# Gate loads in pieces, more load buffers, and sixteen experts kept on the chip, in a two-stage expert layer

## The chip, the cores and the metric

One core of a Trainium2 chip runs the program. The metric is the device time of one execution in microseconds (us). The kernel before took 3175.69 us in the median of three runs (3168.12 to 3179.25).

## The reference

A block of attention, recurrence and a PEER layer is followed by two further blocks (retention and stick-breaking attention, differential attention, each with a convolutional feed-forward part). All is float32, 512 tokens of width 1024. The change touches the PEER layer, which picks per token and head 16 of 16384 experts by two sets of 128 sub-keys:

```python
def block(t):
    q = (t @ wq).reshape(PEER_BLOCK, PEER_HEADS, 2, PEER_DQ // 2)
    s = jnp.einsum('tpcd,pckd->tpck', q, sub_keys).astype(jnp.float32)
    ...
    idx = jnp.take_along_axis(cidx, pos, axis=-1)
    g = jax.nn.softmax(top, axis=-1)
    a = jax.nn.gelu(jnp.einsum('tpkd,td->tpk', u[idx], t).astype(jnp.float32), approximate=False)
    return jnp.einsum('tpk,tpkd->td', (g * a).astype(t.dtype), v[idx])
```

## The kernel before, in words

The kernel doesn't gather for the first 384 tokens (`ND`). It computes all 16384 experts for them and weighs each with its gate, which is zero where the expert isn't picked. An "expert" below is a group of 128 experts; there are 128 of these, numbered 0 to 127. For the last 128 tokens (the "few") the picked rows of both tables are gathered, 128 rows for each table and token, one row per token and transfer: 256 gathers, issued by POOL into four `row` tiles, each with one DVE instruction (L1091 or L1103).

The layer has two stages.

*Hidden stage* (`experts`, `peer_hidden`). For each expert a 512 KB tile of `peer_u` is loaded raw (`wr`) and split into a high and a low float32r half (`wh` by ACT, `wl` by DVE; `wt`, L136). Three products of the halves give one float32 product (`mm3`): 24 matmuls of 128x128 by 128x384. ACT applies gelu (`gl`), and ACT's queue stores the tile of 128 hidden units by 384 tokens in DRAM (`hd`, 192 KB). Beside it the gates are worked out and stored in DRAM (`gd`) in 12 pieces of 32 tokens.

*Output stage* (`peer_out`). For each expert, in order, 192 KB of `hd` come back (`hx`, four buffers), every eighth expert also the gates of eight experts (`gs`, 1536 KB, two buffers). DVE multiplies (`hx<-hx,gs`), ACT and DVE split the product into `ah` and `al` (the trace calls both `ah`), the weights of `peer_v` are loaded and split like those of `peer_u`, and 24 matmuls add to eight accumulators that fill the whole of PSUM. The last three experts' products are kept until the end, where the few's sum is added and the next block's first weights are loaded (`group_start`).

What sets the order: a scheduler reorders the program's instructions ahead of time and gives each engine a fixed list. Each engine, and SP with the loads, works its list strictly in order, so that an instruction that waits holds up all behind it. A load waits until its buffer was read for the last time. Raw weights go round two buffers in the pool `w` and, in this layer, a third in the pool `few`; `wh` and `wl` have three buffers each, and so do `ah` and `al`. The few's DVE instructions are tied behind the split of the weights issued last (`paced`), which spreads them over the experts: 1.15 beside each hidden expert after the fourth, 1 beside each output expert.

Of the kernel before, what the change touches and what calls it, by code (L numbers as in the profile page):

```python
# [9 lines left out]
F32 = mybir.dt.float32  # L10
F32R = mybir.dt.float32r
# [8 lines left out]
P = 128  # L20
T = 512
L = 256
D = 1024
# [8 lines left out]
N2 = T // 2  # L32
TOKENS = (slice(0, N2), slice(N2, T))
SPARSE = 3
ND = 3 * P
HK = 32
HG_LEVELS = [64, 32, 16, 8, 4, 2, 1]
# [27 lines left out]
class Kern:  # L65
    def __init__(self, ctx, tc, A, out):
        self.ctx, self.tc, self.nc, self.A, self.out = ctx, tc, tc.nc, A, out
        self.table, self.epoch, self.later = None, [], []
        self.coming_up, self.ready, self.third, self.turn = [], [], None, 0
        self.pool = lambda name, bufs=1, **k: tc.tile_pool(name=name, bufs=bufs, **k)  # L70
        self.cst = ctx.enter_context(self.pool("cst"))
        self.wp = ctx.enter_context(self.pool("w"))
        self.hp = ctx.enter_context(self.pool("h"))
        self.sp = ctx.enter_context(self.pool("scr"))
        self.dp = ctx.enter_context(self.pool("dram", space=bass.MemoryType.DRAM))
        self.pp = ctx.enter_context(self.pool("ps", space=PSUM))
        self.psb = dict(mm=2, a=4, o=2)
# [58 lines left out]
    def wt(self, src):  # L136

        nc, n = self.nc, src.shape[-1]
        self.turn = (self.turn + 1) % 3
        third = self.third if self.turn == 0 else None  # L140
        raw = (third or self.wp).tile([P, 1024], F32, name="wr", tag="wr", bufs=1 if third else 2)[:, :n]
        hi = self.wp.tile([P, 1024], F32R, name="wh", tag="wh", bufs=3)[:, :n]
        lo = self.wp.tile([P, 1024], F32R, name="wl", tag="wl", bufs=3)[:, :n]
        nc.sync.dma_start(out=raw, in_=src)
        self.mark = self.split(raw, hi, lo)
        return hi, lo
# [776 lines left out]
    def peer_best(self, t, vals, idx):  # L923
# [59 lines left out]
        nc.vector.reciprocal(out=sm, in_=sm)  # L983
        if t != SPARSE:
            nc.vector.tensor_scalar(out=sm, in0=sm, scalar1=1024.0, scalar2=None, op0=ALU.mult)
# [3 lines left out]
    def peer_pick(self, t, vals, idx):  # L989
# [15 lines left out]
        return at, wt  # L1005

    def peer_gates(self, t, at, wt, gp, between):

        nc = self.nc
# [30 lines left out]
    def peer_hidden(self, e):  # L1040

        def evac(ps):
            g = self.fp.tile([P, ND], F32, name="gl", tag="gl", bufs=2)
            self.act(out=g, in_=ps, func=AF.Gelu)
            self.nc.scalar.dma_start(out=self.hd[e], in_=g)
        self.proj_t(self.A["peer_u"][e], [[x[:, :ND] for x in y] for y in self.h], evac, ND)

    def few_rows(self):

        nc = self.nc  # L1050
        tok = slice(ND, T)
        self.hn = self.fp.tile([P, D], F32, name="hn")
# [9 lines left out]
    def few_pick(self, vals, idx):  # L1062
        nc = self.nc
        ci = self.peer_best(SPARSE, vals, idx)
        self.few_i = self.fp.tile([P, P], U32, name="few_i")
# [45 lines left out]
    def peer(self):  # L1111
        nc, A = self.nc, self.A
        self.gd = self.dp.tile([ND // HK, P, P, HK], F32, name="gd")
        self.hd = self.dp.tile([P, P, ND], F32, name="hd")
        with self.pool("few") as self.fp:
            with self.pool("rt") as self.rt:
                self.iota = self.rt.tile([P, P], F16, name="iota")
                nc.scalar.dma_start(out=self.iota, in_=A["iota"])
                self.steps = self.rt.tile([P, 3, 16, 2], F16, name="steps")
                nc.scalar.dma_start(out=self.steps, in_=A["steps"])  # L1120
                vals, idx = self.peer_route()
                done, taken, few = [0], [0.0], iter(())

                def some(n):
                    taken[0] += n
                    while taken[0] >= 1:
                        taken[0] -= 1
                        next(few, None)

                def experts(upto):  # L1130
                    while done[0] < min(upto, P):
                        self.peer_hidden(done[0])
                        done[0] += 1
                        some(1.15)
                experts(4)
                self.few_rows()
                self.few_pick(vals, idx)
                few = self.few_experts()
                self.third = self.fp
                store = []  # L1140
                with self.pool("gp") as gp:
                    for t in range(3):
                        for k in range(4 if t else 10):
                            experts(done[0] + 1)
                            if store:
                                store.pop(0)()
                        at, wt = self.peer_pick(t, vals, idx)
                        base = done[0]
                        store = self.peer_gates(t, at, wt, gp, lambda k, base=base: experts(base + (28 * k) // P))
                    for k in range(4):  # L1150
                        experts(done[0] + 1)
                        store.pop(0)()
                experts(P)
            with self.pool("pv") as pv:
                self.peer_out(pv, few, some)

    def peer_out(self, pv, few, some):

        nc, A = self.nc, self.A
        acc = [self.ps(t) for t in ("a", "a", "a", "a", "o", "o", "mm", "mm")]  # L1160
        last = []
        for e in range(P):
            if e % 8 == 0:
                gs = pv.tile([P, ND // HK, 8, HK], F32, name="gs", tag="gs", bufs=2)
                nc.sync.dma_start(out=gs, in_=self.gd[:, :, e:e + 8, :].rearrange("t p i k -> p t i k"))
            h = pv.tile([P, ND], F32, name="hx", tag="hx", bufs=4)
            nc.sync.dma_start(out=h, in_=self.hd[e])
            w = self.wt(A["peer_v"][e])
            h4 = h.rearrange("p (t k) -> p t k", k=HK)
            self.mul(h4, h4, gs[:, :, e % 8, :])  # L1170
            a = [pv.tile([P, ND], F32R, name="ah", tag=t, bufs=3) for t in ("ah", "al")]
            self.split(h, *a)
            some(1.0)
            if e >= P - 3:
                last.append((w, a))
                continue
            for m in range(KD):
                self.mm3(acc[m][:, :ND], [(self.part(w, m), a)], start=e == 0, stop=False)
        self.run(few)
        self.third = None  # L1180
        self.h = self.htiles()
        s2 = self.scr("acc", T, 1)
        self.group_start([A["w_even"][i] for i in (16, 20, 17, 21)],
                         [[pv.tile([P, T], F32R, name="we", tag=t, bufs=4) for _ in range(4)] for t in ("we", "hx")])
        def column(m, c):
            x = self.x[m][:, c]
            d = slice(c.start, min(c.stop, ND))
# [611 lines left out]
```

## Time and profile before

| | |
|---|---|
| median of three runs | 3175.69 us |
| profiled execution | 3168.37 us, of which the span 3166.3 |
| PE busy | 3036.1 us, 96% |
| DVE, ACT, POOL busy | 70%, 46%, 13% |
| granted TensorE clock, mean | 0.981 |
| DMA over the span | 554.65 MB, 175 GB/s |
| last hidden gelu, first output matmul | 1281.5 us, 1280.5 us |
| last output matmuls before the kept three | 1857 us |

PE is TensorE's matmul, DVE is VectorE, ACT is ScalarE, SP is the engine whose queue issues the loads. An idle engine matters only where another waits for it. The granted clock is 1 at 2.4 GHz and 0.5 at 1.2 GHz.

### The profile page before, as it was taken

Reading aid. Unit: us, or ns where it says so; the run is one execution under the profiler, and the core shown is the slowest. Engines: PE = TensorE matmul, PEld = TensorE weight load, DVE = VectorE, ACT = ScalarE, POOL = GpSimd, SP = SyncE. Lnnn points to the kernel's source line nnn. Section 1 sums busy time; section 2 is a strip of 40 time slices with the busy share of each in tenths; the row PEclk is TensorE's granted clock in tenths of the full one; section 3 lists DMA queues with packets and bytes.
Section 4 is the critical chain, followed back from the end, with each engine's and each line's share of the span. In section 5 each row is a group of like instructions: output and inputs, shape, how many; then the busy total and the mean of one; then the engine's idle time right before and its main releaser. Section 6 shows DMA issues by size and latency. Waiting matters only on the chain.

```text
span 3166.3 us, 46312 instructions
## 1 busy us (share of the span) xinstructions
PE 3036.1 (96%) x17608; PEld 2740.4 (87%) x17608; DVE 2214.9 (70%) x4302; ACT 1465.6 (46%) x2291; POOL 399.0 (13%) x387
## 2 busy tenths in 40 slices
PE   7999999997999999999989999999999999999998
PEld 4998888887999998999989999778888887888887
DVE  7677767898988975677767664668664477786644
ACT  5654465333444443333333345766443277664433
POOL 0001210013333332222223100000000000000000
PEclk9999999998999999999999999999999999999999
DMA  6202444348989999988889832122333322223232
GB/s 221 67 28 81 144 159 134 103 147 286 330 326 343 338 354 349 317 304 308 312 290 322 272 115 80 60 61 84 98 99 93 94 86 79 77 76 99 93 98 82
DMA packets 199326, 554.65 MB, mean 175 GB/s; under 512 B 21280, under 2 KB 82208, under 8 KB 199104
## 3 DMA queue, kind: packets, MB, share of 16 engines
q1 hardware_dynamic: 137200, 376.36, 36.1%
q0 software_dynamic: 42608, 149.06, 13.6%
q10 hardware_dynamic: 19296, 26.28, 2.3%
q8 instruction: 138, 2.26, 0.3%
q14 instruction: 84, 0.69, 0.1%
HBM read 497.61 MB, written 54.00 MB: 174 GB/s over the span
## 4 chain that ended last, share of the span: by engine, by line
PE 64%; DMA 14%; DVE 14%; ACT 5%; issue 3%; SPq 0%; POOL 0%; DVEq 0%; ACTq 0%; POOLq 0%
PE mm L183 48%; DMA hx<-hd 8%; PE a L186 6%; PE a L183 4%; DVE wl L121 4%; PE o L186 2%; PE o L183 2%; DMA wr<-in_peer_u 2%; DVE row L1091 1%; ACT wh L109 1%; DMA wr<-in_w_mod 1%; ACT L105 1%; DMA wr<-in_peer_v 1%; DVE few_y L1103 1%; DVE ah L121 1%
## 5 line engine op out<-in xcount | busy, mean ns | idle before, releaser
L109 ACT ACTIVATE wh<-wr 128x1024 fp32r<-128x1024 f32 (+1 forms) x508 | 531.9, 1048 | 1068.5 <-PE mm L183 830.7
L121 DVE TENSOR_TENSOR wl<-wr,wh 128x1024 fp32r<-128x1024 f32 (+1 forms) x508 | 613.7, 1208 | 384.2 <-ACT wh L109 380.8
L183 PE MATMUL mm<-hh,wh 128*128 128x512 f32 (+2 forms) x2248 | 821.1, 368 | 23.2 <-ACT gl L109 20.6
L183 PE MATMUL mm<-hh,wl 128*128 128x512 f32 (+2 forms) x2216 | 806.4, 364 | 14.1 <-DVE wl L121 14.1
L183 PE MATMUL mm<-hl,wh 128*128 128x512 f32 (+2 forms) x2184 | 791.7, 363 | 0.0
L183 PEld LDWEIGHTS mm<-hh,wh 128*128 128x128 f32 x2248 | 426.4, 190 | 68.7 <-ACT gl L109 23.6
L183 PEld LDWEIGHTS mm<-hh,wl 128*128 128x128 f32 x2216 | 420.2, 190 | 59.2 <-DVE wl L121 16.6
L183 PEld LDWEIGHTS mm<-hl,wh 128*128 128x128 f32 x2184 | 414.1, 190 | 39.9 <-issue 1.0
L183 PE MATMUL a<-ah,wh 128*128 128x384 f32 (+1 forms) x1030 | 273.0, 345 | 34.3 <-DVE ah L121 34.3
L183 PE MATMUL mm<-ah,wh 128*128 128x384 f32 (+2 forms) x920 | 278.5, 349 | 1.0 <-DVE x L1239 1.0
L1084 POOL DMA_INDIRECT row<-in_peer_rows,few_i x128 | 167.9, 1312 | 570.1 <-DVE few_a L1091 255.5
L183 PE MATMUL mm<-ah,wl 128*128 128x512 f32 (+2 forms) x658 | 232.4, 353 | 0.0
L183 PEld LDWEIGHTS a<-ah,wh 128*128 128x128 f32 x1030 | 192.5, 194 | 38.9 <-DVE ah L121 38.5
L1084 POOL DMA_INDIRECT row<-in_peer_v,few_i x128 | 168.1, 1313 | 387.5 <-DVE few_y L1103 262.5
L121 DVE TENSOR_TENSOR hx<-hx,gs 128x384 f32<-128x384 f32 x128 | 71.0, 556 | 163.7 <-DMA hx<-hd 163.2
L183 PEld LDWEIGHTS mm<-ah,wh 128*128 128x128 f32 x920 | 171.2, 191 | 13.5 <-DVE x L1239 1.4
L183 PE MATMUL a<-ah,wl 128*128 128x384 f32 (+1 forms) x515 | 177.3, 344 | 0.0
L1103 DVE SCALAR_TENSOR_TENSOR few_y<-row,few_a,few_y 128x1024 f32<-128x1024 f32 x127 | 162.4, 1279 | 0.2
L1091 DVE CUSTOM_DVE_ANT_0 row<-row,hn 128x1024 f32<-128x1024 f32 x128 | 155.4, 1218 | 6.8 <-DMA row<-in_peer_rows,few_i 6.6
L183 PE MATMUL mm<-al,wh 128*128 128x512 f32 (+1 forms) x396 | 145.1, 366 | 0.0
L183 PE MATMUL o<-ah,wh 128*128 128x384 f32 (+2 forms) x524 | 135.9, 341 | 0.0
L183 PEld LDWEIGHTS mm<-ah,wl 128*128 128x128 f32 x658 | 124.9, 190 | 12.0
(491 smaller groups left out, 5554.0 us busy)
## 6 DMA issues: line engine op xcount, KB each, us to landing
wr<-in_peer_u SPq DMA_DIRECT2D x128, 512.0 KB
wr<-in_peer_v SPq DMA_DIRECT2D x128, 512.0 KB
wr<-in_w_up SPq DMA_DIRECT2D x88, 512.0 KB
hd<-gl ACTq DMA_DIRECT2D x128, 192.0 KB
gd<-gst SPq DMA_DIRECT2D x48, 512.0 KB
gs<-gd SPq DMA_DIRECT2D x16, 1536.0 KB
hx<-hd SPq DMA_DIRECT2D x128, 192.0 KB
wr<-in_w_mod SPq DMA_DIRECT2D x32, 512.0 KB
```

Source lines behind the costliest of these rows:

```text
L105: load = ins(self.nc.scalar.preload_act_table_set(name))
L109: i = ins(self.nc.scalar.activation(out=out, in_=in_, func=func, **k))
L121: return self.nc.vector.tensor_tensor(out=out, in0=a, in1=b, op=op)
L183: self.nc.tensor.matmul(ps, x, y, start=start and i == 0 and j == 0, stop=stop and i == n - 1 and j == 2, **kw)
L186: self.nc.tensor.matmul(ps, a, b, start=start, stop=stop, **k)
L1084: nc.gpsimd.indirect_dma_start(out=r, out_offset=None, in_=table, in_offset=bass.IndirectOffsetOnAxis(ap=self.few_i[:, k:k + 1], axis=0))
L1091: self.paced(nc.vector.tensor_tensor_reduce(out=r, in0=r, in1=self.hn, scale=1.0, scalar=0.0, op0=ALU.mult, op1=ALU.add, accum_out=dots[:, ...
L1103: self.paced(nc.vector.scalar_tensor_tensor(out=self.few_y, in0=r, scalar=dots[:, k:k + 1], in1=self.few_y, op0=ALU.mult, op1=ALU.add))
```

## The change

Gates: the first tile of eight experts is still loaded at once; each later one is loaded in four pieces of three token groups, issued in the program beside the fifth to eighth expert of the group before. The `hx` tile has six buffers instead of four. In the output stage raw weights go round four buffers, the fourth in the pool `pv`. The gelu outputs of experts 112 to 127 stay in a pool `hold` (16 tiles of 192 KB) and aren't stored or loaded; the output stage takes these 16 first, then 0 to 111. The next block's first weights go to the gathers' `row` tiles. The sum over experts is thus taken in another order, with the same terms.

```diff
     def wt(self, src):
...
-        self.turn = (self.turn + 1) % 3
-        third = self.third if self.turn == 0 else None
-        raw = (third or self.wp).tile([P, 1024], F32, name="wr", tag="wr", bufs=1 if third else 2)[:, :n]
+        pools = [self.wp, self.wp] + self.raws
+        pool = pools[self.turn % len(pools)]
+        self.turn += 1
+        raw = pool.tile([P, 1024], F32, name="wr", tag="wr", bufs=pools.count(pool))[:, :n]
...
     def peer_hidden(self, e):
 
         def evac(ps):
-            g = self.fp.tile([P, ND], F32, name="gl", tag="gl", bufs=2)
+            keep = e >= P - HELD
+            g = (self.hold if keep else self.fp).tile([P, ND], F32, name="gl", tag="gl", bufs=HELD if keep else 2)
             self.act(out=g, in_=ps, func=AF.Gelu)
-            self.nc.scalar.dma_start(out=self.hd[e], in_=g)
+            if keep:
+                self.held[e] = g
+            else:
+                self.nc.scalar.dma_start(out=self.hd[e], in_=g)
...
-                self.third = self.fp
+                self.raws = [self.fp]
...
+                experts(P - HELD)
+            with self.pool("hold") as self.hold:
                 experts(P)
-            with self.pool("pv") as pv:
-                self.peer_out(pv, few, some)
+                with self.pool("pv") as pv:
+                    self.peer_out(pv, few, some)
...
-        for e in range(P):
-            if e % 8 == 0:
-                gs = pv.tile([P, ND // HK, 8, HK], F32, name="gs", tag="gs", bufs=2)
-                nc.sync.dma_start(out=gs, in_=self.gd[:, :, e:e + 8, :].rearrange("t p i k -> p t i k"))
-            h = pv.tile([P, ND], F32, name="hx", tag="hx", bufs=4)
-            nc.sync.dma_start(out=h, in_=self.hd[e])
+        self.raws = [self.fp, pv]
+        order = list(range(P - HELD, P)) + list(range(P - HELD))
+        gates = {}
+
+        def gate_parts(p, ts):
+
+            if p not in gates:
+                gates[p] = pv.tile([P, ND // HK, 8, HK], F32, name="gs", tag="gs", bufs=2)
+            e = order[p]
+            nc.sync.dma_start(out=gates[p][:, ts], in_=self.gd[ts, :, e:e + 8, :].rearrange("t p i k -> p t i k"))
+        gate_parts(0, slice(0, ND // HK))
+        for p, e in enumerate(order):
+            if p % 8 > 3 and p + 8 < P:
+                gate_parts(p // 8 * 8 + 8, slice(p % 4 * 3, p % 4 * 3 + 3))
+            gs = gates[p // 8 * 8]
+            h = self.held.get(e)
+            if h is None:
+                h = pv.tile([P, ND], F32, name="hx", tag="hx", bufs=6)
+                nc.sync.dma_start(out=h, in_=self.hd[e])
             w = self.wt(A["peer_v"][e])
...
         self.group_start([A["w_even"][i] for i in (16, 20, 17, 21)],
-                         [[pv.tile([P, T], F32R, name="we", tag=t, bufs=4) for _ in range(4)] for t in ("we", "hx")])
+                         [[t[:, j * T:(j + 1) * T] for t in [self.fp.tile([P, D], F32R, name="we", tag="row", bufs=4) for _ in range(2)] for j in range(2)]
+                          for _ in range(2)])
```

How this moves instructions is shown at three places. Numbers behind names tell tiles apart; lines are those of the file each list comes from (a line after L136 of the old file has a higher number in the new one).

The first place is DVE's list where the first output products stand among the last hidden experts. Before, `hx_13106` is expert 0, `wl_12454` the split of hidden expert 111 and `wl_12491` that of 112:

```order
L121 TENSOR_TENSOR hx_13106<-hx_13106,gs_13104 128x384
L121 TENSOR_TENSOR wl_12454<-wr_12452,wh_12453 128x1024
L1091 ISA row_12486,few_a_6821<-row_12486,hn_6648 128x1024
L1091 ISA few_a_6821 128x1
L121 TENSOR_TENSOR ah_13116<-hx_13106,ah_13115 128x384
L121 TENSOR_TENSOR hx_13146<-hx_13146,gs_13104 128x384
L121 TENSOR_TENSOR hx_13186<-hx_13186,gs_13104 128x384
L121 TENSOR_TENSOR hx_13226<-hx_13226,gs_13104 128x384
L121 TENSOR_TENSOR wl_12491<-wr_12489,wh_12490 128x1024
```

In the changed list `wl_12606` is hidden expert 115, `gl_12524` the kept tile of 112:

```order
L122 TENSOR_TENSOR wl_12606<-wr_12604,wh_12605 128x1024
L1109 SCALAR_TENSOR_TENSOR few_y_6822<-row_12639,few_a_6821,few_y_6822 128x1024
L122 TENSOR_TENSOR gl_12524<-gl_12524,gs_13091 128x384
L122 TENSOR_TENSOR ah_13101<-gl_12524,ah_13100 128x384
L122 TENSOR_TENSOR gl_12560<-gl_12560,gs_13091 128x384
```

and later `gl_12781` is the kept tile of 119, the last to use the first gate tile `gs_13091`; `hx_13711`, `hx_13751` and `hx_13793` are experts 0 to 2 with the third gate tile `gs_13554`, and `wl_12971` is hidden expert 125:

```order
L122 TENSOR_TENSOR gl_12781<-gl_12781,gs_13091 128x384
L122 TENSOR_TENSOR wl_12899<-wr_12897,wh_12898 128x1024
L1109 SCALAR_TENSOR_TENSOR few_y_6822<-row_12930,few_a_6821,few_y_6822 128x1024
L122 TENSOR_TENSOR gl_12817<-gl_12817,gs_13245 128x384
L122 TENSOR_TENSOR wl_12935<-wr_12933,wh_12934 128x1024
L1109 SCALAR_TENSOR_TENSOR few_y_6822<-row_12966,few_a_6821,few_y_6822 128x1024
L122 TENSOR_TENSOR gl_12856<-gl_12856,gs_13245 128x384
L122 TENSOR_TENSOR hx_13711<-hx_13711,gs_13554 128x384
L122 TENSOR_TENSOR hx_13751<-hx_13751,gs_13554 128x384
L122 TENSOR_TENSOR hx_13793<-hx_13793,gs_13554 128x384
L122 TENSOR_TENSOR wl_12971<-wr_12969,wh_12970 128x1024
```

The first product moved from ahead of the split of 111 to behind that of 115; three products of later experts now stand ahead of the split of 125.

The second place is DVE's list in the middle of the output stage. Before, `ah_13396` is the low half of expert 7, `hx_13508` the product of expert 10 and `wl_13432` the weights of expert 8:

```order
L121 TENSOR_TENSOR ah_13396<-hx_13386,ah_13395 128x384
L1091 ISA row_13399,few_a_6821<-row_13399,hn_6648 128x1024
L1091 ISA few_a_6821 128x1
L121 TENSOR_TENSOR hx_13508<-hx_13508,gs_13426 128x384
L121 TENSOR_TENSOR wl_13432<-wr_13430,wh_13431 128x1024
L121 TENSOR_TENSOR ah_13438<-hx_13428,ah_13437 128x384
```

After, `ah_13761` is the low half of expert 1, `hx_13957` the product of expert 6 and `wl_13797` the weights of expert 2:

```order
L122 TENSOR_TENSOR ah_13761<-hx_13751,ah_13760 128x384
L1109 SCALAR_TENSOR_TENSOR few_y_6822<-row_13766,few_a_6821,few_y_6822 128x1024
L122 TENSOR_TENSOR hx_13957<-hx_13957,gs_13554 128x384
L122 TENSOR_TENSOR wl_13797<-wr_13795,wh_13796 128x1024
L122 TENSOR_TENSOR ah_13803<-hx_13793,ah_13802 128x384
```

Behind the split of expert e stands the product of e+3 before and of e+5 now.

The third place is SP's list in the output stage. Before, `hx_13428` and `hx_13468` are experts 8 and 9, `wr_13430` and `wr_13470` their weights, `gs_13748` the gates of 16 to 23:

```order
L1167 DMA hx_13428<-hd_5653 128x384
L1165 DMA gs_13748<-gd_5652 128x12x256
L144 DMA wr_13430<-in_peer_v 128x1024
L1167 DMA hx_13468<-hd_5653 128x384
L144 DMA wr_13470<-in_peer_v 128x1024
```

After, `hx_14038` and `hx_14078` are experts 8 and 9, `wr_13959`, `wr_14000` and `wr_14040` the weights of 6, 7 and 8, `gs_14198` the gates of 16 to 23:

```order
L146 DMA wr_13959<-in_peer_v 128x1024
L1189 DMA hx_14038<-hd_5653 128x384
L1180 DMA gs_14198<-gd_5652 128x3x256 x2
L146 DMA wr_14000<-in_peer_v 128x1024
L1189 DMA hx_14078<-hd_5653 128x384
L1180 DMA gs_14198<-gd_5652 128x3x256 x2
L146 DMA wr_14040<-in_peer_v 128x1024
```

Between the same two hx, the whole gate tile stood before and two of its pieces stand now, the other two behind the next hx; weights follow one expert later behind hx.

## Rows read from the trace of the kernel before

**Rows 1.** The page's part 2: busy tenths in 40 slices of the span.

```profile
PE   7999999997999999999989999999999999999998
...
DMA  6202444348989999988889832122333322223232
```

**Rows 2.** Stretches: from:to, length, busy of PE PEld DVE ACT POOL, clock, DMA share, GB/s.

```profile
1183.00:1280.50 97.50, 90.31 (x509) 89.36 (x509) 58.77 (x66) 32.08 (x46) 27.92 (x25) 0.98 0.98 349
1280.50:1372.00 91.50, 88.37 (x499) 87.73 (x499) 64.25 (x92) 30.90 (x43) 19.43 (x21) 0.98 0.90 309
1372.00:1760.00 388.00, 357.62 (x1977) 354.11 (x1975) 269.39 (x360) 122.20 (x168) 97.97 (x82) 0.96 0.89 308
1760.00:1857.00 97.00, 96.21 (x538) 95.96 (x539) 63.86 (x83) 35.00 (x48) 7.93 (x6) 0.96 0.67 218
```

**Rows 3.** Chain that ended last, late output stage: start, us, what.

```profile
1776.23 2.08 PE a L183 x12
...
1780.39 2.08 PE a L183 x12
```

**Rows 4.** Waits from 1280 to 1857: total us, times, longest.

```profile
DVE hx L121 <- DMA hx<-hd: 148.3, 57, 9.8
ACT wh L109 <- DMA wr<-in_peer_v: 95.4, 24, 9.2
...
PE a L183 <- DVE ah L121: 34.3, 13, 5.2
```

**Rows 5.** SP's queue of transfers in time: start, us to issue, engine, what.

```profile
1332.45 0.37 SPq L1165 DMA_DIRECT2D gs<-gd  x1
1333.59 1.16 SPq L144 DMA_DIRECT2D wr<-in_peer_v  x1
1334.80 1.17 SPq L1167 DMA_DIRECT2D hx<-hd  x1
...
1347.73 0.33 SPq L144 DMA_DIRECT2D wr<-in_peer_v  x1
```

**Rows 6.** Chain that ended last, output stage: waits for hx alone.

```profile
1334.80 11.12 DMA hx<-hd
1355.49 5.27 DMA hx<-hd
1362.97 5.01 DMA hx<-hd
...
1746.19 12.36 DMA hx<-hd
```

**Rows 7.** DVE in time; in brackets the idle time before.

```profile
1338.11 0.55 DVE L121 TENSOR_TENSOR ah<-hx,ah 128x384 fp32r<-128x384 f32 x1
...
1346.01 0.56 DVE L121 TENSOR_TENSOR hx<-hx,gs 128x384 f32<-128x384 f32 x1 [6.20 <-DMA hx<-hd]
1346.48 1.22 DVE L121 TENSOR_TENSOR wl<-wr,wh 128x1024 fp32r<-128x1024 f32 x1
```

**Rows 8.** Stretches as in rows 2: DMA share and GB/s at the end.

```profile
1100.00:1180.00 80.00, 80.00 (x557) 78.58 (x556) 63.06 (x69) 33.87 (x53) 28.36 (x21) 1.00 0.96 346
...
1334.00:1343.00 9.00, 9.00 (x54) 9.00 (x53) 4.48 (x8) 2.95 (x4) 1.87 (x2) 1.00 1.02 360
1346.00:1350.00 4.00, 2.63 (x15) 2.31 (x15) 3.99 (x7) 0.29 (x1) 0.42 (x1) 1.00 0.40 107
1355.00:1374.00 19.00, 19.00 (x111) 19.00 (x110) 16.82 (x21) 7.24 (x11) 4.83 (x5) 1.00 0.98 337
```

**Rows 9.** Waits from 1183 to 1280.5, the last hidden experts.

```profile
DVE hx L121 <- DMA hx<-hd: 14.8, 3, 8.8
...
PE mm L183 <- ACT gl L109: 7.2, 3, 3.7
```

**Rows 10.** Transfers of hx: issue time in ns, min/median/max, first and last.

```profile
L1167 SPq DMA_DIRECT2D hx<-hd x128: 319/341/2008, 1191.6 to 1841.4; - x128
```

**Rows 11.** What SP's queue waited for, 1280.5 to 1760.

```profile
SPq L144 <- DVE wl L121: 318.0, 90, 11.4
```

More of the change, by code (lines that the diff above doesn't have):

```diff
@@ L34 @@
 SPARSE = 3
+HELD = 16
 ND = 3 * P
@@ L68, in __init__ @@
         self.table, self.epoch, self.later = None, [], []
-        self.coming_up, self.ready, self.third, self.turn = [], [], None, 0
+        self.coming_up, self.ready, self.raws, self.turn = [], [], [], 0
         self.pool = lambda name, bufs=1, **k: tc.tile_pool(name=name, bufs=bufs, **k)
@@ L1113, in peer @@
         self.gd = self.dp.tile([ND // HK, P, P, HK], F32, name="gd")
-        self.hd = self.dp.tile([P, P, ND], F32, name="hd")
+        self.hd = self.dp.tile([P - HELD, P, ND], F32, name="hd")
+        self.held = {}
         with self.pool("few") as self.fp:
@@ L1173, in peer_out @@
             some(1.0)
-            if e >= P - 3:
+            if p >= P - 3:
                 last.append((w, a))
@@ L1177, in peer_out @@
             for m in range(KD):
-                self.mm3(acc[m][:, :ND], [(self.part(w, m), a)], start=e == 0, stop=False)
+                self.mm3(acc[m][:, :ND], [(self.part(w, m), a)], start=p == 0, stop=False)
         self.run(few)
-        self.third = None
+        self.raws = []
         self.h = self.htiles()
```

## Prediction

> **What bounds the kernel now.** I read the page first. PE is busy 96% of the span; its slices say 9 nearly everywhere, and from the tenth to the 23rd of 40 the DMA slices say 8 or 9 as well [rows 1]. In that part lies what the change touches; so I cut it by stretches: the last hidden experts (1183 to 1280.5 us), and the output experts in three pieces up to 1857 [rows 2]. In the output stage one expert costs PE 24 matmuls, and where nothing disturbs it the pattern comes back after 1780.39 - 1776.23 = 4.16 us [rows 3]. 125 experts run in it (three are kept for the end): 125 x 4.16 = 520 us, but it takes 576.5. The excess of about 56 us is the stake. The stretches say the same: idle PE is 3.1 + 30.4 + 0.8 = 34.3 us, and the granted clock of 0.98, 0.96 and 0.96 takes 0.02 x 91.5 + 0.04 x 388 + 0.04 x 97 = 21.2 us more; together 55.5. The last hidden experts lose 7.2 us idle and 0.02 x 97.5 = 1.9 us of clock [rows 2]. All that this change touches is worth at most 55.5 + 9.1 = 64.6 us.
>
> What the lost time waits for is in the list of waits: PE waits 34.3 us for the split of the hidden activations on DVE, and DVE waits 148.3 us, 57 times, for hx, the hidden activations that come back from DRAM; ACT waits 95.4 us for raw weights [rows 4]. The queue of SP tells why hx is late: a gate load of 1.5 MiB is issued at 1332.45, a weight load behind it, and hx behind both at 1334.80 [rows 5]. It is landed 11.1 us later; between two gate loads it takes 5.0 to 5.3 [rows 6]. DVE stands still for 6.20 us, and the weights' split behind it, for which PE waits next, stands too [rows 7]. From the first such pair of gate load and late hx to the last is 1746.19 - 1334.80 = 411.4 us for 11 groups of eight experts: 37.4 us a group, where PE alone wants 8 x 4.16 = 33.3.
>
> While DVE stands, nothing is issued: the next weights go out at 1347.73, nine us after the pair before [rows 5], and the DMA engines fall from a share of 1.02 and 360 GB/s to 0.40 and 107 [rows 8]. The stage is thus not short of bandwidth all the time; it runs full, then empty.
>
> **The change part by part.** Per output expert the transfers are 524 KB of raw weights, 197 of hx, 1573 / 8 = 197 of gates and 524 of gathered rows, 1.44 MB. At 4.16 us that is 347 GB/s. Between 1100 and 1180 the same engines moved 346 GB/s with PE busy all the 80 us [rows 8]. So PE's own pace can just be fed, if the engines never run empty. That is the knife's edge of this forecast.
>
> *Held experts.* 16 stores and 16 loads of hx go away, 3.1 MB each way, and the stage begins with the experts whose activations are in SBUF, with six hx already loaded. The first 22 experts need no hx in time; they want 1.25 MB in 4.16 us, 299 GB/s, below what any saturated row shows. They run at PE's pace and cover 22 x 4.16 = 91.5 us, just the length of the second stretch, which loses 3.1 + 1.8 = 4.9 us now. Gain 5.
>
> *The passage from hidden to output experts.* Before, DVE stood for hx for 14.8 us among the last hidden experts, and PE lost 7.2 us to a gelu queued behind [rows 9]. The order shows the first gate product moved from ahead of expert 111's weight split to behind 115's, some 16 us later, when its gate tile, issued at the same place, has landed. New are three hx products ahead of expert 125's split; they need the third gate tile, whose pieces can go out only after the eighth held product, about two experts before. Its 1.57 MB and one weight load are 2.1 MB beside gathers of 126 GB/s (524 KB each 4.16 us): 2.1 MB at 360 - 126 = 234 GB/s is 9 us, and the two experts are 8.3. So DVE may stand 1 to 4 us, with what a load takes to land, but PE needs that split only two experts later. On the other side two gate tiles, a weight load and six hx (4.9 MB) now sit in SP's queue among hidden experts 112 to 117 where 4.5 MB sat. I take 4 of the 9.1 us as staying (bounds 0 and 9.1). Gain 5.
>
> *Six buffers for hx.* The order eats them: before, the product of expert e+3 stood behind the split of e, now that of e+5 does. hx still goes out when one split is done and is wanted after the next; the slack is one expert, as before. I give this part nothing.
>
> *The fourth raw buffer.* Weights go out four experts ahead instead of three, 4.16 us more slack. The 95.4 us of ACT [rows 4] mostly lie beside DVE's wait for hx, so by itself I price it at nothing; it keeps work in the queue while DVE stands.
>
> *Gates in pieces.* Two pieces each go out behind two successive hx, 786 KB a time, instead of 1573 KB once. hx then has 2.2 us (at 360 GB/s) ahead of it twice, not 4.4 once. More to the point, when the first delayed hx lands, the second pair of pieces and a weight load are still queued, 1.3 MB or 3.6 us of work, so that the hole of [rows 8] should close. Group time: between gate loads DVE goes through two experts in 1362.97 - 1355.49 = 7.48 us, 3.75 each [rows 6], DVE's limit with hx in time; eight of them and the gates' full 4.4 us make 34.4 us, 1.1 above PE's 33.3. Of 256 gathers, 1.15 went beside each of 124 hidden experts, so that they run out near the 113th output expert, and 92 experts, 11.5 groups, remain behind the first 22: 13 us idle. DVE enters with the lead that three buffers for split weights allow, two experts or 8.3 us, and that covers most of it: 5 us. Clock has cost 21.2 us to 34.3 idle, 0.62 each, so 5 to 13 idle become 8 to 21 us. I take 11, nearer the end with the lead. Now the third and fourth stretch lose 30.4 + 15.5 + 0.8 + 3.9 = 50.6: gain 40. Ends: nothing lost (gain 50.6) and, with the group at 37.4 still, no gain.
>
> 45 more gate transfers are issued (1 + 15 x 4 against 16), 16 hx fewer. An issue takes SP 0.34 us, 2.0 at most [rows 10], and SP waited 318 us of that stage for DVE's splits [rows 11]: hidden.
>
> The Trainium skill ("DMA: Bandwidth & Descriptors", Rules for kernel authors) asks for at least 1 MiB per DMA, and its Anatomy section fits 2.0 us fixed per transfer; pieces of 384 KiB go against that, and 45 of them in line would be 90 us (an estimate from that page). In the stretch from 1355 to 1374, which has no transfer above 512 KiB, the engines moved 337 GB/s [rows 8], so that the fixed part evidently overlaps here; by this the pieces cost 1573 KB x (1/337 - 1/360) = 0.3 us a group.
>
> *Behind the stage* the first weights of the next block go into the gather buffers instead of hx buffers; these are free when the gathers end, 50 us before. Nothing.
>
> **Sum.** The profiled execution took 3168.4 us (span 3166.3 and 2.1 around). 3168.4 - 5 - 5 - 40 = 3118.4. The median shown, 3175.7, lies 7.3 above it; if that comes from this stage it goes, if from elsewhere it stays. I add half: 3122.
>
> **Rivals.**
> 1. *Smoother, but still short of data* (0.25). 347 GB/s is wanted throughout and the output stretches had 308; mixed with gates of 1 KB runs the engines may not hold it, and DVE, in order, still meets each hx one expert after its issue. A group comes half way, 35.4 us: 50.6 becomes 20 of gain, 3168.4 - 30 + 4 = 3142.
> 2. *The pieces do nothing* (0.11). hx waits for as many bytes, twice half instead of once the whole, and the group stays at 37.4. Only held experts and the passage gain: 3168.4 - 10 + 4 = 3162. Against it: the hole of [rows 8].
> 3. *Slower* (0.06). Each added piece holds SP's queue ahead of weights and hx. If each costs there the 2.0 us of the longest issue seen [rows 10], 45 x 2.0 = 90 against 50 of gain: 3168.4 + 40 + 4 = 3212. It decides from 1.3 us apiece; against it stand the 0.34 median and SP's long waits. The fixed part on that page of the Trainium skill would give the same.
>
> **How the numbers follow.** The forecast has 0.58, with a range of its own from 3106 (losses gone but for a little) to 3138 (the lead unused and no gain in the passage). Least thinkable is 3168.4 - 64.6 = 3104. The range goes from there into the second rival, to 3155; outside remain most of the cases of 3162 and the slower one. A change of under 0.3%, 9.5 us, can't be told from none here. Faster: the forecast, rival 1 and a third of rival 2, 0.87; same 0.07; slower 0.06.
>
> **What would show it.** Right: from 1280 on PE steps of 4.16 us over 22 experts; a stage of 520 to 535 us; DVE's wait for hx at single waits of some 3 us instead of 6 to 10; no stretch of DMA share 0.4; clock at 1.0 nearly throughout; before 1183 us and behind the stage nothing new. Wrong: groups of 36 us or more with the DMA share at 0.95 (rival 1), with holes still there (rival 2), or SP busy issuing while DVE and ACT wait for weights (rival 3). The forecast falls altogether if the wait moves to the gathers, which DVE hardly waited for, or if the passage loses more than now.

## The result, and the profile after

The changed kernel takes 3132.9 us (median of four runs, 3130.9 to 3135.4), against 3175.2 for the kernel before on the same chip: a ratio of 0.9861, 95% interval 0.9840 to 0.9882. That is faster by 42 us, or 1.3%, and lies in the predicted range of 3104 to 3155, 11 us above the predicted 3122. The profiled execution took 3133.6 us, its span 3131.6. The gap of 7.3 us between profile and median of before is not there.

In the page's slices the columns are as in [rows 1]:

```profile
PE   7999999998999999999999999999999999999998
...
DMA  6212454238989999899999722222333232223332
```

In the output stage the DMA slices are now 9 from the 18th to the 22nd, where four of these five were 8. The stage by stretches, cut as in [rows 2] but at this kernel's own bounds (the stage runs from 1281.8 to 1821.6 us, 539.7 us against 576.4):

```profile
1183.00:1281.50 98.50, 93.98 (x530) 92.85 (x529) 64.19 (x76) 33.26 (x48) 31.24 (x24) 0.98 0.92 335
1281.50:1373.00 91.50, 91.50 (x530) 91.50 (x528) 66.55 (x92) 32.57 (x45) 23.89 (x23) 1.00 0.91 313
1373.00:1725.00 352.00, 340.37 (x1939) 336.68 (x1939) 266.03 (x355) 120.81 (x165) 87.79 (x81) 1.00 0.94 329
1725.00:1822.00 97.00, 95.84 (x551) 95.06 (x550) 61.89 (x79) 34.06 (x47) 5.71 (x6) 1.00 0.65 214
```

The second stretch now has PE busy without a gap at clock 1.00, where [rows 2] had 88.37 of 91.50 at 0.98. The third keeps an idle rest of 352 - 340.37 = 11.6 us (30.4 before) and the clock is 1.00 where it was 0.96. DMA share and rate rose from 0.89 and 308 GB/s to 0.94 and 329. The waits from 1281.5 to 1822 (total us, times, longest) answer to [rows 4]:

```profile
DVE hx L122 <- DMA hx<-hd: 102.5, 63, 4.4
...
PE a L185 <- DVE ah L122: 12.7, 12, 2.5
```

DVE's wait for hx fell from 148.3 to 102.5 us, and its longest from 9.8 to 4.4; the 95.4 us of ACT for raw weights are gone from the list, ACT now waits for PE (313.7 us); PE's own wait fell from 34.3 to 12.7. So the change did what it says, and did not finish: hx is still late, and the transfers still run empty at times, if seldom (columns as in [rows 2], against the 0.40 and 107 GB/s of [rows 8]):

```profile
1628.00:1632.00 4.00, 3.12 (x18) 2.80 (x17) 4.00 (x5) 1.93 (x4) 0.39 (x1) 1.00 0.31 77
```

SP's queue in a group of eight shows why hx is late (start, us to issue, what), beside [rows 5]:

```profile
1457.65 0.91 SPq L1180 DMA_DIRECT2D gs<-gd  x2
1458.79 0.35 SPq L146 DMA_DIRECT2D wr<-in_peer_v  x1
1459.25 0.60 SPq L1189 DMA_DIRECT2D hx<-hd  x1
1459.90 1.76 SPq L1180 DMA_DIRECT2D gs<-gd  x2
1462.15 0.34 SPq L146 DMA_DIRECT2D wr<-in_peer_v  x1
1462.61 0.35 SPq L1189 DMA_DIRECT2D hx<-hd  x1
```

All four pieces go out within 4 us, in two pairs, each pair with a weight load ahead of the next hx. In the program they belong to four successive experts; in SP's list, as the third place above shows, they stand two and two around a weight load and an hx, and they go out once the gate buffer comes free. The hx of 1462.61 lands 11.2 us later, just as long as in [rows 6], and DVE stands for it (in brackets the idle time before):

```profile
1473.90 0.56 DVE L122 TENSOR_TENSOR hx<-hx,gs 128x384 f32<-128x384 f32 x1 [4.33 <-DMA hx<-hd]
```

4.33 us instead of the 6.20 of [rows 7], but still in every group: from the 24th output expert's split to the 112th, eleven groups of eight, the trace has 386.2 us, 35.1 each (37.45 by the same count before).

Where the 34.7 us of span came from: the stage gave 36.7, the passage ahead of it 3, the first hidden expert's gelu came 4.5 us later in this execution than in the one of before, and what lies behind the stage took 0.6 us more. These are the two rows (kernel before, then after; first and last start stand at the end of the time columns), 628.9 us from first to last gelu before and 625.7 after:

```profile
L109 ACT ACTIVATE gl<-mm x128: 466/472/512, 652.6 to 1281.5; 128x384 f32<-128x384 f32 x128
```

```profile
L110 ACT ACTIVATE gl<-mm x128: 467/472/510, 657.1 to 1282.8; 128x384 f32<-128x384 f32 x128
```

Nothing that the change touches lies ahead of that first gelu; in the thirteen profiled executions here it comes between 649.6 and 658.5 us. Such a difference of a few us says nothing of the change, and stages are compared below instead of spans.

### The profile page after: what moved, and what is told of

The parts are those of the page before. It is cut to its first block, busy times and chain, and to the rows that moved or that the text cites. A ratio compares the mean times of both kernels' runs of the same rounds, so it can differ in the third digit from the quotient of the medians.

```text
span 3131.6 us, 46209 instructions
## 1 busy us (share of the span) xinstructions
PE 3023.7 (97%) x17608; PEld 2725.8 (87%) x17608; DVE 2216.3 (71%) x4302; ACT 1466.5 (47%) x2291; POOL 394.1 (13%) x387
## 3 DMA queue, kind: packets, MB, share of 16 engines
q1 hardware_dynamic: 135616, 373.22, 36.3%
## 4 chain that ended last, share of the span: by engine, by line
PE 71%; DMA 12%; DVE 10%; ACT 5%; issue 2%; POOL 0%; DVEq 0%; SPq 0%; ACTq 0%
PE mm L185 52%; PE a L188 7%; DMA hx<-hd 7%; PE a L185 5%; DVE wl L122 3%; PE o L185 3%; PE o L188 3%; DMA wr<-in_peer_u 1%; ACT wh L110 1%; DMA wr<-in_w_mod 1%; ACT L106 1%; DMA gs<-gd 1%; DVE ah L122 1%; DMA row<-in_peer_rows,few_i 1%; DVE row L1097 0%
## 5 line engine op out<-in xcount | busy, mean ns | idle before, releaser
L185 PE MATMUL a<-ah,wh 128*128 128x384 f32 (+1 forms) x1030 | 265.4, 336 | 12.8 <-DVE ah L122 12.7
L1090 POOL DMA_INDIRECT row<-in_peer_v,few_i x128 | 164.5, 1285 | 384.0 <-DVE few_y L1109 272.2
L185 PEld LDWEIGHTS a<-ah,wh 128*128 128x128 f32 x1030 | 186.7, 189 | 17.5 <-DVE ah L122 16.9
L1109 DVE SCALAR_TENSOR_TENSOR few_y<-row,few_a,few_y 128x1024 f32<-128x1024 f32 x127 | 162.5, 1280 | 0.4 <-DMA row<-in_peer_v,few_i 0.3
L122 DVE TENSOR_TENSOR hx<-hx,gs 128x384 f32<-128x384 f32 x112 | 62.2, 558 | 109.9 <-DMA hx<-hd 102.5
L185 PE MATMUL mm<-wh,hl 128*128 128x256 f32 x464 | 133.3, 287 | 0.0
```

The source lines that it names most:

```text
L122: return self.nc.vector.tensor_tensor(out=out, in0=a, in1=b, op=op)
L185: self.nc.tensor.matmul(ps, x, y, start=start and i == 0 and j == 0, stop=stop and i == n - 1 and j == 2, **kw)
L1090: nc.gpsimd.indirect_dma_start(out=r, out_offset=None, in_=table, in_offset=bass.IndirectOffsetOnAxis(ap=self.few_i[:, k:k + 1], axis=0))
L1109: self.paced(nc.vector.scalar_tensor_tensor(out=self.few_y, in0=r, scalar=dots[:, k:k + 1], in1=self.few_y, op0=ALU.mult, op1=ALU.add))
```

## Experiments

The first four take the change apart. The other seven test why hx is late and what it costs. Each was timed beside the kernel before, whose median was 3172.1 to 3175.9 us; kernels are therefore compared by their ratios to it. Stages are read from one profiled execution each. A common ruler for the stage is the stretch from 1400 to 1700 us, in which PE, if never kept waiting, is busy 300 us at clock 1.00 (columns as in [rows 2]); in the kernel before, and then in the changed one, it reads

```profile
1400.00:1700.00 300.00, 277.02 (x1525) 274.47 (x1524) 209.93 (x289) 94.56 (x130) 75.63 (x64) 0.95 0.88 306
```

```profile
1400.00:1700.00 300.00, 289.13 (x1646) 285.85 (x1645) 227.57 (x311) 101.66 (x139) 71.83 (x69) 0.99 0.94 327
```

**Pieces alone.** The kernel before, with only the gates' loads cut:

```diff
+        gate_parts(0, slice(0, ND // HK))
...
-            if e % 8 == 0:
-                gs = pv.tile([P, ND // HK, 8, HK], F32, name="gs", tag="gs", bufs=2)
-                nc.sync.dma_start(out=gs, in_=self.gd[:, :, e:e + 8, :].rearrange("t p i k -> p t i k"))
+            if e % 8 > 3 and e + 8 < P:
+                gate_parts(e // 8 * 8 + 8, slice(e % 4 * 3, e % 4 * 3 + 3))
+            gs = gates[e // 8 * 8]
```

> The kernel before with the gates in four pieces and nothing else changed: no held experts, four hx buffers, three raw buffers. Theory (smaller gate loads close the hole in the transfers): a group of eight output experts falls from 37.4 us to about the 35.1 of the changed kernel, over some 12 groups 25 to 28 us, so 3147 to 3150, between 3140 and 3158; DVE's wait for hx falls from 148 to about 105 us. Rival 1 (the fourth raw buffer made the gain): with three raw buffers it stays above 3165. Rival 2 (the held experts made it, by 3.1 MB less each way and a lead): also above 3165.

Measured 3146.3 us, ratio 0.9914 (0.9896 to 0.9933). Its waits in the output stage:

```profile
ACT wh L109 <- DMA wr<-in_peer_v: 98.2, 29, 5.9
...
PE a L183 <- DVE ah L121: 16.9, 15, 2.2
```

The pieces alone halve PE's wait (34.3 to 16.9) and leave ACT's wait for raw weights where it was. DVE's wait for hx fell to 123.5 us, less far than the 105 expected; the group came to about 35 us as expected, and the stage to 546.6 from 576.4. The pieces alone thus give some 29 of the 42 us.

**The rest without the pieces.** The changed kernel with whole gate loads:

```diff
-            if p % 8 > 3 and p + 8 < P:
-                gate_parts(p // 8 * 8 + 8, slice(p % 4 * 3, p % 4 * 3 + 3))
+            if p % 8 == 0:
+                gate_parts(p, slice(0, ND // HK))
```

> The changed kernel with each gate tile loaded whole again, ahead of the first expert of its group; held experts, six hx buffers and four raw buffers stay. Theory: the first 22 experts still run at PE's pace and the groups behind go back to about 37.4 us, so that some 25 of the 42 us are lost: 3155 to 3160. Rivals 1 and 2 (raw buffer or held experts): 3135 to 3142, and groups stay near 35 us.

Measured 3150.1 us, 0.9928 (0.9910 to 0.9945), 17 us above the changed kernel, some 25 below before, and below the expected range: held experts and buffers give more than expected. The parts don't add up, 29 and 25 against 42 for both, so that the pieces are worth 29 us put in first and 17 put in last.

```profile
DVE hx L122 <- DMA hx<-hd: 113.2, 52, 8.6
...
PE a L185 <- DVE ah L122: 22.6, 12, 3.6
```

hx's longest wait is 8.6 us again, as it is with whole gates; the group is 36.3 us.

**Three raw buffers.**

```diff
-        self.raws = [self.fp, pv]
+        self.raws = [self.fp]
```

> The changed kernel with three raw weight buffers instead of four. Theory: weights were late only behind a whole gate tile; the time stays at 3133 to 3138. Rival 1 (the fourth raw buffer made the gain): ACT's wait for raw weights returns to some 95 us and the time to 3150 or more.

Measured 3137.8 us, 0.9881 (0.9859 to 0.9903).

```profile
ACT wh L110 <- DMA wr<-in_peer_v: 90.7, 27, 6.4
...
PE a L185 <- DVE ah L122: 11.7, 9, 2.0
```

ACT's wait comes back to 90.7 us, and PE's stays at 11.7. A long wait of an engine that another wait covers is worth little: 5 us at most, with intervals that overlap, and 2 us of stage (541.9 against 539.7).

**Four hx buffers.**

```diff
-                h = pv.tile([P, ND], F32, name="hx", tag="hx", bufs=6)
+                h = pv.tile([P, ND], F32, name="hx", tag="hx", bufs=4)
```

> The changed kernel with four hx buffers instead of six. Theory: DVE's order uses up the buffers, each hx is still wanted one expert after its issue, and the time stays at 3133, within 4 us. Rival (six buffers give hx the slack): DVE's wait for hx goes back towards 148 us and the time to 3145 or more.

A miss: 3123.6 us (3123.2 to 3126.0), 0.9841 (0.9823 to 0.9860), faster than the changed kernel in every single run. By the medians the two more buffers had cost 9 us; the intervals of the two ratios overlap a little, but the stage says the same, 532.4 against 539.7 us, and PE's wait in it fell from 12.7 to 6.8. DVE's wait for hx did not go up:

```profile
DVE hx L122 <- DMA hx<-hd: 95.1, 71, 5.0
```

SP's queue of this kernel in a group with pieces:

```profile
1463.57 0.34 SPq L146 DMA_DIRECT2D wr<-in_peer_v  x1
1464.04 0.53 SPq L1189 DMA_DIRECT2D hx<-hd  x1
1464.62 1.45 SPq L1180 DMA_DIRECT2D gs<-gd  x2
1468.40 0.33 SPq L1189 DMA_DIRECT2D hx<-hd  x1
1468.77 6.38 SPq L146 DMA_DIRECT2D wr<-in_peer_v  x2
```

Behind the second pair of pieces hx now goes ahead of its weight load (1468.40), where the changed kernel had a weight load between (1462.15, 1462.61). In the chain that ended last the late hx of the changed kernel reads, and then that of this one:

```profile
1462.61 11.19 DMA hx<-hd
```

```profile
1468.40 8.83 DMA hx<-hd
```

524 KB less ahead of it, and 2.4 us less from issue to landing in this pair; 1.1 of these are lost again, as hx was issued 3.8 us behind the second pair of pieces here and 2.7 us behind it there. Six buffers move the hx loads two experts up the list, past the weights of their own expert, without giving them more time before use. That the two orders differ so is shown; that this alone makes the 9 us is inferred, and the next runs bear on it.

**Is it the burst of pieces or the mean rate?** The four pieces of a group tied each behind another expert's hx load:

```diff
+            g = nc.sync.dma_start(out=gates[p][:, ts], in_=self.gd[ts, :, e:e + 8, :].rearrange("t p i k -> p t i k"))
+            if hx:
+                self.after(getattr(g, "ins", g), hx[-1])
...
-            if p % 8 > 3 and p + 8 < P:
-                gate_parts(p // 8 * 8 + 8, slice(p % 4 * 3, p % 4 * 3 + 3))
+            if p % 2 and p + 8 < P:
+                gate_parts(p // 8 * 8 + 8, slice(p % 8 // 2 * 3, p % 8 // 2 * 3 + 3))
```

> The changed kernel, but the four pieces of a gate tile are tied each behind the gelu load of another expert, so that one piece goes out every second expert, where in the changed kernel all four go out within two experts. Theory A (the burst of pieces makes two experts of each eight late, by 7 us in place of 4.16): the late experts vanish, groups 33.3 to 34.2 us, time 3113 to 3123. Theory B (the mean data rate binds, about 335 GB/s, wherever the pieces stand): groups 34.4 to 35.1, time 3123 to 3133.

Measured 3113.8 us, 0.9808 (0.9784 to 0.9831). SP's queue now has one piece for two experts, and the stretch from 1400 to 1700 and the waits read:

```profile
1456.93 0.42 SPq L1180 DMA_DIRECT2D gs<-gd  x1
...
1460.77 0.53 SPq L1191 DMA_DIRECT2D hx<-hd  x1
...
1465.50 0.34 SPq L1191 DMA_DIRECT2D hx<-hd  x1
1465.89 0.62 SPq L1180 DMA_DIRECT2D gs<-gd  x1
```

```profile
1400.00:1700.00 300.00, 299.08 (x1724) 298.44 (x1724) 235.28 (x319) 106.75 (x147) 84.58 (x72) 1.00 0.96 340
```

```profile
DVE hx L122 <- DMA hx<-hd: 82.1, 70, 4.4
...
PE a L185 <- DVE ah L122: 1.1, 3, 0.6
```

PE waits 1.1 us where it waited 12.7, at 340 GB/s. DVE still waits 82.1 us for hx, but only two of the waits in the stage are over 2.8 us, where the changed kernel has twelve. The mean rate was no limit; the burst was, for a product that wants its load one expert after its issue.

**The same with four hx buffers** (both edits above).

> The same spread pieces with four buffers for gelu outputs in place of six. Four buffers with the pieces close together gave 3123.6 against 3132.9 with six. If the fewer buffers are worth 9 us by themselves, this is some 9 us below the spread kernel with six; if they only changed how the pieces' burst met the other loads, both are the same within 3 us: 3113 to 3121.

Measured 3115.6 us, 0.9804 (0.9780 to 0.9828): the same as with six.

```profile
1400.00:1700.00 300.00, 300.00 (x1732) 300.00 (x1732) 241.38 (x323) 107.67 (x147) 78.66 (x72) 1.00 0.97 347
```

```profile
DVE hx L122 <- DMA hx<-hd: 60.2, 64, 3.3
```

This is less of a test than it was meant to be. With the pieces spread PE already runs at its own pace with six buffers (299.08 of 300 us busy), so that nothing was left to gain; and DVE's wait for hx did fall, from 82.1 to 60.2 us. That fewer buffers help only by how the burst meets the other loads fits the time, but isn't shown.

**Is it the place of the product?** The changed kernel with each gate product placed behind the split of its own expert's weights on DVE:

```diff
-            self.mul(h4, h4, gs[:, :, e % 8, :])
+            self.paced(self.tt(h4, h4, gs[:, :, e % 8, :], ALU.mult))
```

> The changed kernel, but each product of a gelu output with its gates is placed behind the split of its own expert's weight tile on VectorE, so that a gelu load has some six experts between issue and use in place of one. Theory A (each late load is a load wanted one expert after its issue, because the product stands early in VectorE's order): VectorE's waits for gelu loads nearly vanish (102.5 us in the changed kernel, under 30 here), the groups of eight come to 33.5 to 34.2 us, the time to 3117 to 3124 us. Theory B (the stage's data rate is the limit, the waits only show it): the waits go elsewhere, groups stay at 35.1, time 3130 to 3136. A third outcome, slower than 3136, if the later product, which also frees the gate tile later, makes the gate pieces late.

Measured 3113.3 us, 0.9802 (0.9779 to 0.9824), lower than either theory's range. DVE's wait for hx is not in the list any more, and no wait for raw weights is over 1.2 us in the stage:

```profile
ACT ah L110 <- DVE hx L122: 209.0, 110, 2.2
```

```profile
1400.00:1700.00 300.00, 300.00 (x1733) 300.00 (x1732) 240.96 (x323) 116.29 (x148) 73.53 (x72) 1.00 0.97 348
```

ACT now waits 209 us for the products, 2.2 at a time at most, DVE waits for ACT's halves in turn (91.2 us from 1282 to 1800), and PE waits for neither: it is busy for all of the 300 us. The stage takes 523.6 us, 125 x 4.16 + 3.6.

**Nothing held.** The constant HELD at 0 in the changed kernel.

> The changed kernel with no held gelu outputs (the constant 16 set to 0): all 128 are stored and loaded again, experts in the order 0 to 127. Theory: the stage loses its lead of some 46 experts without a gap (the first gap comes within the first group of eight), and the loads that the 16 experts add are 3 MiB, some 9 us at 337 GB/s: 3141 to 3147 us. Rival: the held tiles only change where the data is and the groups of eight stay the limit all the same: 3131 to 3136.

Measured 3145.9 us, 0.9912 (0.9887 to 0.9937): the time as expected, the reason not. PE's first gap in the stage comes at 1415, not in its first group, and the stage takes 538.8 us, as with held experts. What is lost lies ahead of it:

```profile
L110 ACT ACTIVATE gl<-mm x128: 467/472/510, 651.8 to 1290.6; 128x384 f32<-128x384 f32 x128
```

```profile
1183.00:1280.00 97.00, 84.26 (x450) 83.23 (x449) 54.21 (x61) 29.04 (x42) 25.25 (x22) 0.91 0.94 339
1400.00:1700.00 300.00, 288.71 (x1647) 284.68 (x1646) 225.29 (x307) 101.78 (x140) 85.51 (x68) 1.00 0.94 330
```

```profile
DVE hx L122 <- DMA hx<-hd: 17.9, 6, 8.6
...
PE mm L185 <- ACT gl L110: 12.7, 3, 5.5
```

638.8 us from first to last gelu, against 625.7: DVE stands for hx among the hidden experts, gelus queue behind, PE is busy 84 of 97 us at clock 0.91. Held experts pay in the passage, by keeping early products from waiting for loads there. That holds for this kernel, with its six hx buffers and its pieces: the kernel before, with nothing held either, took 628.9 us between the same gelus and lost 7.2 us there [rows 9].

**The kernel before with the late product alone.** One line, all else as before (whole gates, four hx buffers, three raw buffers, nothing held):

```diff
-            self.mul(h4, h4, gs[:, :, e % 8, :])
+            self.paced(self.tt(h4, h4, gs[:, :, e % 8, :], ALU.mult))
```

> The kernel before (whole gates, four buffers for gelu outputs, three raw weight buffers, nothing held) with one edit: each product of a gelu output with its gates is placed behind the split of its own expert's weight tile on VectorE. Theory A (the loads were late because the product stands three experts ahead in VectorE's order, so that a load is wanted one expert after its issue): with some four experts between issue and use an expert late by 11 us is covered, the groups of eight fall from 37.4 to 33.3 to 34.5 us, the time to 3120 to 3135 us, most of what the whole change gives, and more. Theory B (whole gates hold up the loads behind them whatever the order): groups stay above 36.5, time 3160 or more.

Measured 3113.1 us (3111.8 to 3118.0), 0.9813 (0.9788 to 0.9839): faster than the changed kernel by 20 us, and faster than theory A had it. From 1285 on:

```profile
1285.00:1400.00 115.00, 115.00 (x666) 115.00 (x665) 91.28 (x126) 44.06 (x57) 28.32 (x28) 1.00 0.97 342
1400.00:1700.00 300.00, 300.00 (x1732) 300.00 (x1731) 241.44 (x325) 114.78 (x148) 72.73 (x72) 1.00 0.98 349
```

```profile
ACT ah L109 <- DVE hx L121: 217.9, 115, 2.2
...
ACT wh L109 <- DMA wr<-in_peer_v: 25.9, 13, 2.9
```

PE runs through without a gap at 349 GB/s. SP still waits for DVE before it sends hx, but DVE's list now has each product just behind the split of its own expert's weights. From its issue to the start of its product an hx load has 14.4 us here (median, loads issued from 1400 to 1700), against 5.4 in the kernel before, 5.7 in the changed kernel and 5.5 in the same with four buffers. A late load's 11 us fit into the 14.4, and not into the others. In the changed kernel the late product gives 22.7 us with six buffers and 14.4 with four: buffers buy time once the product is late, and none before.

The late product also evens out SP's queue. In the changed kernel with it, weights and hx go out in turn every 2.1 us (1445.00, 1447.08, 1449.16 and on). How much of the cure is the time until use and how much the even issue, these runs don't separate.

**Late product with whole gates, and with four hx buffers**, each on the changed kernel.

> The changed kernel with whole gates (one load of 1.5 MiB for eight experts) and the late product. Whole gates cost the changed kernel 17 us (3150 against 3133). Theory A: with some six experts of slack the size of the gate load no longer matters: 3112 to 3118 us, as with pieces and the late product (3113). Theory B: a whole gate load still holds up the loads queued behind it: 3122 to 3130.

> The changed kernel with the late product and four buffers for gelu outputs in place of six. Theory A (with the late product every buffer is an expert of slack, but four are enough for pieces of 384 KiB): 3112 to 3118 us. Rival (six buffers are needed once the order lets them be used): 3119 or more.

Measured 3114.9 us, 0.9812 (0.9782 to 0.9841), and 3108.6 us, 0.9803 (0.9777 to 0.9829). The stretch of the second:

```profile
1400.00:1700.00 300.00, 300.00 (x1733) 300.00 (x1732) 240.93 (x324) 115.90 (x147) 73.38 (x72) 1.00 0.97 348
```

Neither size of gate load nor number of buffers moves the stage once the product is late (523.6 us in both, 348 GB/s). The last is the fastest kernel here by its median, below both kernels of the case; the 4.7 us to the late product with six buffers are not resolved by the intervals.

## Why the prediction was right, and by what it was off

- **The bound, the stake and the sign: right.** DVE standing for hx behind a gate load set the pace, and 52.8 of the stake of 55.5 us in the stage can be had: it falls from 576.4 to 523.6 us as soon as PE no longer waits.
- **The knife's edge of 347 GB/s: right that it can be fed.** 347 to 349 GB/s ran for 300 us in five kernels. [rows 2] could have said so ahead: 349 GB/s over 97.5 us among the last hidden experts. Rival 1 had two reasons. The first, that the engines may not hold the rate, falls: the changed kernel's 329 GB/s was what the loads that had been issued in time came to. The second, that DVE still meets each hx one expert after its issue, is what the runs show, and the rival's 35.4 us a group is nearer to the measured 35.1 than the forecast's 34.4.
- **Held experts: right in sum, mis-sized in place.** The gain of 5 in the stage's first 91.5 us came as forecast, and the lead lasted to 1473 us, 46 experts and not 22. But with nothing held the stage is no longer, and its first gap still comes late; the 13 us that holding is worth in this kernel lie in the passage.
- **The passage: mis-sized, 5 against 3, and not where it was looked for.** DVE stood 6.9 us for the third gate tile, where the prediction had 1 to 4 us:

```profile
1266.84 1.50 DVE L122 TENSOR_TENSOR hx<-hx,gs 128x384 f32<-128x384 f32 x3 [6.86 <-DMA gs<-gd]
```

As the prediction said, PE hardly felt that: of the 4.5 us that it still waits from 1183 to 1281.5, 0.6 are behind this split, and the rest comes sooner and from a late gelu:

```profile
PE mm L185 <- ACT gl L110: 3.9, 2, 3.7
```

- **Gates in pieces: the term that was mis-sized.** The forecast had 34.4 us a group, a rest of 11 us and a gain of 40; measured are 35.1, a rest of 19.7 over 520, and 36.7 for the whole stage, the held experts' 5 included. The step that failed is "2.2 us ahead of it twice, not 4.4 once": the two pairs go out within one expert's time, so that their second hx has a whole gate load's bytes and two weight loads issued within the 5 us ahead of it, and takes 11.2 us as before. The other term of the 34.4 was misread as well. The 3.75 us an expert were called DVE's limit, but in [rows 6] the chain runs through a load of 5.27 us within these two experts' 7.48; where DVE had work to make up (kernel before with the late product), it took 3.37 us from split to split:

```profile
1458.96 1.22 DVE L121 TENSOR_TENSOR wl<-wr,wh 128x1024 fp32r<-128x1024 f32 x1 [3.04 <-ACT wh L109]
...
1462.33 1.22 DVE L121 TENSOR_TENSOR wl<-wr,wh 128x1024 fp32r<-128x1024 f32 x1
```

With 3.37 the same sum gives 31.4 us a group, below PE's 33.3, and no loss at all. So 34.4 came near 35.1 partly by luck: one term too long and one too short. What did come is that the hole behind mostly closes (longest wait 4.4 instead of 9.8), though a stretch at DMA share 0.31 is still there, and the stage of 539.7 us is past the 520 to 535 named as a sign. Spread evenly, the pieces do what the forecast hoped for: 3113.8.
- **Six hx buffers, priced at nothing: wrong in sign by a little.** The reading of the order was right, one expert of slack before and after, and buffers added no time (5.4 and 5.7 us from issue to use). But I looked at DVE's list alone. In SP's queue the same edit put hx behind weights of earlier experts, and it cost 7 us of stage and 9 of the median with the pieces in a burst.
- **The fourth raw buffer, priced at nothing:** 0 to 5 us.
- **45 more issues: hidden, as said.** Rival 3 falls, since pieces alone gain 29 us. The stretch from 1355 to 1374, from which the prediction takes its 0.3 us a group, isn't free of large transfers: SP issued a gate load at 1368.59, and up to 1368.5 the rate was 326 GB/s, which makes it 0.5. The Trainium skill ("DMA: Bandwidth & Descriptors", Rules for kernel authors) asks for at least 1 MiB per DMA; by the trace neither side of that rule decides here. With products early, small pieces win, as by their order fewer bytes stand ahead of the next load; with products late, whole loads of 1.5 MiB (0.9812) and pieces of 384 KiB (0.9802) are equal. The 2.0 us fixed per transfer that the prediction takes from the Trainium skill (same page, Anatomy of one DMA) is given there for transfers that GpSimd issues; these go out from SP, and no run here shows it as a cost.
- **Sum.** In the profiled execution 3118.4 was forecast and 3133.6 came: 8.3 us of stage, 1.8 of passage, 4.5 of the late first gelu, which varies from run to run, and 0.6 behind. Half of the 7.3 us between profile and median was to stay, and none did; so the median is off by 11 and not by 15, which is luck.
- **What the prediction did not see.** It wrote that the order eats the buffers and took the order as given. PE's loss needs two things together: loads that land late behind a burst, and an order that wants them one expert after their issue. Taking away either one, by spread pieces or by the late product, brings the time to 3109 to 3116 us. A product that stands three or five experts ahead of need on an in-order engine wants its load one expert after its issue, however many buffers there are, and while it waits, the weight splits behind it, which free the buffers for the next loads, wait too. Moving the product changes one line of the kernel before and gives all that the change gave, and 20 us more.

## What to carry to other kernels

Buffers are prefetch depth only as far as the instruction that waits for the load stands late in its engine's order; count the instructions between the one that frees a buffer and the one that wants its next content, and where that distance is short, move the consumer before adding buffers or cutting transfers. Read the queue that issues the loads as well as the engine that waits: loads meant for four steps can go out in one burst, and a deeper buffer can put one load behind another's. A stretch with less than full DMA share beside a stalled in-order engine is no bandwidth limit until the stall is taken away and the rate is read again.

## What the runs showed of the hardware

The DMA engines held 347 to 349 GB/s at a share of 0.97 to 0.98 for 300 us beside a TensorE that never paused, with transfers of 192 KB to 1.5 MB mixed; the kernel before had shown 346 GB/s over 80 us with TensorE busy throughout [rows 8], and 349 over 97.5 us in which TensorE paused [rows 2]. The granted clock, 1 being 2.4 GHz and 0.5 being 1.2, was lower where PE stood idle more. Its mean from 1400 to 1700 us was 0.95 in the kernel before (23.0 us idle, up to 5.2 at a time), 0.99 in the changed kernel (10.9 us, up to 2.5) and 1.00 in the five kernels whose PE never paused. Idle time alone does not settle it: with nothing held the clock was 1.00 as well, at 11.3 us idle. So taking away the waits gave their own 21.6 of the stage's 36.7 us (34.3 to 12.7), and the other 15.1 came off the time in which PE was busy, with the same matmuls and the higher clock.
